# Value projections of the recurrent layers from two-part fp32r products, low weight parts by adding transfers, the inverse transposed into place, and a new order table

## The chip, the cores and the metric

The kernel runs on one core of one Trainium2 chip. The metric is device time in microseconds (us) of one execution; lower is better. The engines that matter are TensorE (PE, matrix products), VectorE (DVE), ScalarE (ACT), GpSimd (POOL) and SyncE (SP, which issues transfers).

## The reference

A residual trunk of four layers over 256 tokens of width 1024. The token mixers are RWKV-7, stick-breaking attention, sparse attention, RWKV-7; a SwiGLU feed-forward layer follows each. The change touches only the two RWKV layers (0 and 3):

```
xm  = h + (shifted - h) * mix                 # six mixes: r, k, v, w, a, g
r, k, v = xm[0:3] @ w_rkv                     # 1024 x 1024 each
decay, a, g from low-rank products of three other mixes
if layer 3: v = v + (v_first - v) * sigmoid(v0 + (xv @ v1) @ v2)
kk  = normalised (k * k_k);  k = k * (1 + (a - 1) * k_a)
state = state * w - (state.kk) (kk * a)^T + v k^T      # per token and head, 16 heads of 64
y     = state . r
out   = (group_norm(y) + (r.k.r_k) v) * g @ w_out
```

All inputs are float32. The recurrence is computed in chunks of 64 tokens.

## The kernel before, in words

The code doesn't issue instructions directly. It records them as operations in a `Plan`, in the order of the Python text. A long compressed table, `ORDER`, then says in which order they are issued over the whole program, which of the "any engine" operations (`anye`) go to DVE, ACT or POOL, and which buffer slot each tile gets. `emit` (line 546, so nearly every instruction carries that line) replays the table. Each engine takes its own instructions strictly in that order and waits at an instruction until its inputs are there. Where the table has an empty entry, `emit` issues `WARMERS` = 2 matmuls into an unused bank, `warm_o<-warm_x` (line 1572, 128x256 in bf16); no result depends on them.

Weights come in pieces of 512 KB (128 partitions x 1024 float32) as tiles `raw`, loaded by SP's queue. `piece` splits a piece into two fp32r tiles: `wh`, a rounding copy on any engine, and `wl = raw - wh`, a subtraction on DVE. `gemm2` multiplies with three fp32r products per tile (`mm3`: wh with the high part of the activations, wh with their low part, wl with the high part). The value projection alone, `vp`, is different before the change: `product` multiplies the float32 `raw` tile directly with the float32 activations `xv`, without any split. Slots are few: three for `wh`, three for `wl`.

An RWKV layer runs in this sequence (names are those of the profile):

- mixes of the normalised input on DVE (`xm`, `xr`, `xg`, `xv`), split into high and low halves (`kx` for keys, `prx` for r);
- key projection `kp` (piece `ahead` is one split earlier), low-rank `lora` products, the decay scan `L`, the r projection `rp`, which gives `PR`;
- `kss`, `ksd`, `kk`: key normalisation; then per pair of heads the scores `sc` on PE, which DVE masks into `SB`;
- `vp`, and from it `vf` (in layer 3 by way of `vd`), then transposes by matmul, `vtok`, and copies of them into `UV` for the products `bv`; `qct` fills `QC`;
- the inverse: eight small copies gather the 32x32 triangular blocks of `SB` into `E`, DVE transposes them into `inv`, and 31 steps of two DVE instructions each (`xtmp<-inv`, `inv<-inv,xtmp`) invert all blocks at once;
- DVE transposes the inverse to `xd` and, the other way, to `xw`; four copies `XT<-xw`, one for each group of 32 partitions, put `xw` into the larger matrix `XT`;
- `combine`: `cmb<-xd,SB` on PE, a copy `zs`, `cmb<-xw,zs` on PE, the result scaled into `XT`. It fills the off-diagonal block of each 64x64 inverse;
- the chain over the chunks (`xu<-u,XT`, `qu`, `pS`, `Y`), then the group norm, the gate (`pg` gives `gT`), and the output projection `po`.

`bn`, `prhl` and `pr` are the bonus term (r.k.r_k), and `am`, `EF`, `dc`, `Dt` belong to the decay.

Of the kernel before, what the change touches and what calls it, by code (L numbers as in the profile page):

```python
# [308 lines left out]
k{-II~7K%FccRBy3x!BJ(c;1U*;dauQ^j|f2=!A8r?36?px_Rwqi64gxnG%9K-
1|M(`IM_!^@WJEdYO4CKM(<b#RY#N`QIx3OuWNi2>Dp>2M_rD`<(N;{LTx`Z&C03Hs`1GJl^F`Ip5!Y^pNj;_mJ=K?N^`hkNClm^WpCd_|_Un93n0u_IoS  # L310
X#ec%~Eu6;|ViW%nv5r_poJDMvI2I6d)oKpsDzliy2&<KR2Gf|LznJ$CJs;B!wj7<oAI_I*HG!2P>Rh?3<3j$U@8KWivW|$NjIX7rOROm+u%u{Pi99<}7-
b^T%uFWZsS_E_IP!+?&&;S9l)~XN`a+{TJ5#4h;ju(K<hYNxi@S7#tu5R{y2ucR%>lxix5nIlpRG8oyQn)orn;;p+w)B(nylVnwHm83cb4_bE#_mP$MU<?
Hp{hG95;$ATgBY0$5_O48uM(01<VP#>jzvhxq=a6h&(9Lv3<s}y2{iLWr?)%$|HF>s-l@<z;_yCRR9llS#x^x1-
# [236 lines left out]
def trunk(ctx: ExitStack, tc: tile.TileContext, xT_in, vecs_in, wts, lora_in, consts_in, id32_in, outT, order, layers=None):  # L550
# [305 lines left out]
    def rwkv(j, layer, after):  # L856
# [39 lines left out]
        def product(key, x, name):  # L896

            out = bank(name, "g")
            for c in range(NC):
                if c % 4 == 0:  # L900
                    w = v3(raw_piece(key + (c // 4,)), 4)
# [833 lines left out]
```

## Time and profile before

| | |
|---|---|
| median of 3 runs | 1363.25 us (1361.84 to 1365.1) |
| the profiled execution | 1361.64 us, span 1359.9 us |
| PE busy | 1347.0 us, 99% of the span |
| DVE busy | 1120.4 us, 82% |
| ACT busy | 759.9 us, 56% |
| POOL busy | 11.4 us, 1% |
| transfers | 221.88 MB, 163 GB/s on average |
| granted PE clock | 1.000 |

Times in the profile count from the start of the span. A row of the timeline gives the start of a run of equal instructions, its length, the engine, line, operation, output and inputs with sizes, the count, and in square brackets how long the engine idled before it and on whose account. Matmuls overlap, so the length of a run of many is a better price than the length of one. A float32 matmul stands in the trace as two records. Layer 0's recurrent part lies at about 12 to 190 us, layer 3's at about 1000 to 1170 us.

### The profile page before, as it was taken

Reading aid. Unit: us, or ns where it says so; the run is one execution under the profiler, and the core shown is the slowest. Engines: PE = TensorE matmul, PEld = TensorE weight load, DVE = VectorE, ACT = ScalarE, POOL = GpSimd, SP = SyncE. Lnnn points to the kernel's source line nnn. Section 1 sums busy time; section 2 is a strip of 40 time slices with the busy share of each in tenths; the row PEclk is TensorE's granted clock in tenths of the full one; section 3 lists DMA queues with packets and bytes.
Section 4 is the critical chain, followed back from the end, with each engine's and each line's share of the span. In section 5 each row is a group of like instructions: output and inputs, shape, how many; then the busy total and the mean of one; then the engine's idle time right before and its main releaser. Section 6 shows DMA issues by size and latency. Waiting matters only on the chain.

```text
span 1359.9 us, 25662 instructions
## 1 busy us (share of the span) xinstructions
PE 1347.0 (99%) x10372; PEld 1179.5 (87%) x10372; DVE 1120.4 (82%) x1881; ACT 759.9 (56%) x1283; POOL 11.4 (1%) x18
## 2 busy tenths in 40 slices
PE   8999999999999999999999999999999999999998
PEld 8887798888888898888999798888897878988887
DVE  7998799775787888776799888876699997988754
ACT  5945566554335666554356965654249465666532
POOL 0000000000000000000000000000002000000000
PEclk9999999999999999999999999999999999999999
DMA  7332166655654367655656456666643321666554
GB/s 248 123 117 94 33 194 210 199 172 158 188 184 139 112 189 220 199 166 170 194 143 191 138 173 197 210 194 204 191 134 122 105 79 50 202 208 201 177 166 131
DMA packets 62854, 221.88 MB, mean 163 GB/s; under 512 B 7312, under 2 KB 8592, under 8 KB 62480
## 3 DMA queue, kind: packets, MB, share of 16 engines
q1 hardware_dynamic: 62736, 220.25, 52.3%
q8 instruction: 81, 1.33, 0.4%
q14 instruction: 37, 0.30, 0.1%
HBM read 217.08 MB, written 1.05 MB: 160 GB/s over the span
## 4 chain that ended last, share of the span: by engine, by line
PE 93%; DVE 3%; DMA 2%; ACT 2%; issue 0%; SPq 0%; DVEq 0%; ACTq 0%
PE dn L546 18%; PE up L546 17%; PE gate L546 17%; PE po L546 7%; PE qk L546 7%; PE vp L546 4%; PE kp L546 3%; PE rp L546 3%; PE vps L546 3%; PE z L546 2%; DMA raw<-in_wts_dram 1%; PE sc L546 1%; PE Y L546 1%; PE attn_o L546 1%; PE pg L546 1%; PE qi L546 1%
## 5 line engine op out<-in xcount | busy, mean ns | idle before, releaser
L546 DVE TENSOR_TENSOR wl<-raw,wh 128x1024 fp32r<-128x1024 f32 x285 | 347.7, 1222 | 98.8 <-ACT wh L546 96.3
L546 ACT CAST wh<-raw 128x1024 fp32r<-128x1024 f32 x237 | 248.7, 1050 | 202.1 <-PE dn L546 111.6
L546 PE MATMUL dn<-h,wh 128*128 128x512 f32 x704 | 244.2, 390 | 0.0
L546 PE MATMUL dn<-h,wl 128*128 128x256 f32 x704 | 198.5, 282 | 0.0
L546 PEld LDWEIGHTS dn<-h,wh 128*128 128x128 f32 x704 | 132.2, 188 | 27.7
L546 PE MATMUL gate<-xg,wring 128*128 128x512 f32 x704 | 133.2, 336 | 1.2 <-DVE wring L546 1.2
L546 PEld LDWEIGHTS dn<-h,wl 128*128 128x128 f32 x704 | 133.0, 189 | 0.0
L546 PE MATMUL up<-xg,wring 128*128 128x512 f32 x704 | 131.9, 336 | 0.0
L546 DVE TENSOR_TENSOR wring<-raw,wring 128x1024 fp32r<-128x1024 f32 x88 | 107.4, 1221 | 27.9 <-ACT wring L546 27.6
L546 PE MATMUL gate<-xg,wh 128*128 128x512 f32 x352 | 125.2, 392 | 0.0
L546 PE MATMUL up<-xg,wh 128*128 128x512 f32 x352 | 125.0, 392 | 0.0
L546 PEld LDWEIGHTS gate<-xg,wring 128*128 128x128 f32 x704 | 107.4, 188 | 16.0 <-DVE wring L546 1.5
L546 PEld LDWEIGHTS up<-xg,wring 128*128 128x128 f32 x704 | 107.4, 188 | 14.6
L546 ACT CAST wring<-raw 128x1024 fp32r<-128x1024 f32 x82 | 86.2, 1051 | 42.6 <-issue 16.5
L546 PE MATMUL gate<-xg,wl 128*128 128x256 f32 x352 | 98.4, 280 | 0.0
L546 PE MATMUL up<-xg,wl 128*128 128x256 f32 x352 | 98.4, 279 | 0.0
L546 PE MATMUL qk<-xg,wh 128*128 128x256 f32 (+1 forms) x384 | 91.5, 320 | 0.0
L546 PEld LDWEIGHTS up<-xg,wh 128*128 128x128 f32 x352 | 66.1, 188 | 14.6
L546 PEld LDWEIGHTS gate<-xg,wh 128*128 128x128 f32 x352 | 66.1, 188 | 14.4
L546 PE MATMUL qk<-xg,wl 128*128 128x256 f32 x256 | 71.7, 280 | 0.0
L546 PEld LDWEIGHTS qk<-xg,wh 128*128 128x128 f32 x384 | 63.5, 188 | 6.1 <-issue 0.8
L546 PEld LDWEIGHTS gate<-xg,wl 128*128 128x128 f32 x352 | 66.1, 188 | 0.0
(322 smaller groups left out, 2623.6 us busy)
## 6 DMA issues: line engine op xcount, KB each, us to landing
raw<-in_wts_dram SPq DMA_DIRECT2D x397, 512.0 KB, 3.7
lora<-in_lora_dram SPq DMA_DIRECT2D x2, 1536.0 KB, 8.3
rhl<-qa SPq DMA_DIRECT2D x32, 64.0 KB, 3.7
xt<-in_xT_dram SPq DMA_DIRECT2D x4, 256.0 KB, 4.3
lora<-in_lora_dram SPq DMA_DIRECT2D x2, 512.0 KB, 5.7
lg<-in_lora_dram SPq DMA_DIRECT2D x8, 128.0 KB, 3.6
inv<-in_id_dram SPq DMA_DIRECT2D x2, 512.0 KB, 3.3
out_dram<-xt SPq DMA_DIRECT2D x4, 256.0 KB, 4.0
```

The lines of the kernel that those rows point to most:

```text
L546: getattr(getattr(nc, o.eng), method)(*map(real, args), **{k: real(a) for k, a in kw.items()})
```

## The change

1. The value pieces are split as the others are. `wh` is the rounding copy as before. For keys in `ADDED`, `wl` isn't subtracted on DVE: ACT (or another engine) writes -wh into it, and a transfer issued by POOL reads the same piece from memory once more and adds it into `wl`. That is 16 transfers of 512 KB. The subtraction stays for all other weights.
2. `vp` uses `gemm2`, three fp32r matmuls in place of one float32 matmul: 384 matmuls in place of 128, which the trace counts as 256 records.
3. `xv` becomes two fp32r tiles, high and low. Each of the 16 mixes (128x256) is written to a scratch `xm`, then copied rounded into the high half and subtracted by DVE into the low half. The low half takes the slot group of `XT`, so `XT` is filled after the last use of `xv`.
4. `xw` goes. DVE transposes `inv` straight into the right-hand columns of `XT` (`XT<-inv`), the second `combine` product reads those columns, and two copies `XT<-XT` in place of four `XT<-xw` fill the left-hand columns.
5. In the code the value projection stands ahead of the inverse.
6. A new `ORDER` for the whole program. Besides order, it changes which engine has some of the free operations, and has 42 warming pairs for 30 (84 `warm_o` for 60).

```
+ADDED = ("rv",)
...
-c-rk+$&aK*R<9Q?wr|bMFTY$Xx5}(sYRjt1%-Z*^s;=&K@7-><-L?m}8{5N-
+c-rk+NpoY#aYokq>g@~ml^_-ZBtZZq2!a6j?q*L<uQR={XXy!PMl+*vNR};23RzM(!V#XZV-DU<KKky1BYd)NKIkX-U-
...
         anye.copy(h, r)
+        if key[0] in ADDED:
+            anye.scale(l, r, -1.0)
+            pool.dma_start(l, wts[i], accum_op=ALU.add)
+            return h, l
         dve.tensor_tensor(l, r, f(h), op=ALU.subtract)
...
-        xv = T([NC, S], "s1", "xv")
+        xv = [T([NC, S], g, "xv", F32R) for g in ("s1", "s0")]
...
             for i in range(c, c + 2):
-                mix(xv[:, i], "mv", i)
-                xvs.append(xv[:, i])
+                xvs.append(xm("mv", i))
+                split(xv[0][:, i], xv[1][:, i], xvs[-1])
...
-            vp = product(("rv", j, n), xv, "vp")
+            vp = gemm2(("rv", j, n), lambda c: (xv[0][:, c], xv[1][:, c]), "vp")
...
         dve.transpose(xd.rearrange("p u i -> p i u"), XI.rearrange("p t i -> p i t"))
-        xw = T([32, 32], "wh", "xw")
-        dve.transpose(xw.rearrange("p u t -> p t u"), XI)
-        for g in (1, 3, 0, 2):
-            r = slice(g * 32, (g + 1) * 32)
-            anye.copy(XT[r, :, g % 2 * 32:g % 2 * 32 + 32], xw[r])
+        dve.transpose(XT[:, :, 32:].rearrange("p u t -> p t u"), XI)
+        for r in (slice(0, 32), slice(64, 96)):
+            anye.copy(XT[r, :, :32], XT[r, :, 32:])
...
-                                  xr_[hi:hi + 32, c], start=True, stop=True)
+                                  X[hi:hi + 32, c, 32:], start=True, stop=True)
```

(`scale(l, r, -1.0)` is recorded with the source `raw` and an fp32r output, so it holds the rounded piece with its sign turned.)

On DVE, at the end of layer 0's inverse, this stands before:

```order
L546 COPY UV<-vtok 64x2x256
L546 TENSOR_TENSOR xtmp<-inv 128x112
L546 TENSOR_TENSOR inv<-inv,xtmp 128x4x28
L546 TENSOR_TENSOR xtmp<-inv 128x87
L546 TENSOR_TENSOR inv<-inv,xtmp 128x3x29
L546 TENSOR_TENSOR xtmp<-inv 128x60
L546 TENSOR_TENSOR inv<-inv,xtmp 128x2x30
L546 TENSOR_TENSOR xtmp<-inv 128x31
L546 TENSOR_TENSOR inv<-inv,xtmp 128x31
L546 TENSOR_TENSOR pr<-bn,vf_1119 128x512
L546 STREAM_TRANSPOSE xd<-inv 128x32x32
L546 STREAM_TRANSPOSE xw<-inv 128x32x32
```

and this now:

```order
L552 TENSOR_SCALAR prs<-pr,vecs 128x256
L552 TENSOR_TENSOR inv<-inv,xtmp 128x4x28
L552 TENSOR_TENSOR xtmp<-inv 128x87
L552 TENSOR_TENSOR inv<-inv,xtmp 128x3x29
L552 TENSOR_TENSOR xtmp<-inv 128x60
L552 TENSOR_TENSOR inv<-inv,xtmp 128x2x30
L552 TENSOR_TENSOR xtmp<-inv 128x31
L552 TENSOR_TENSOR pr<-bn,vf_1283 128x512
L552 TENSOR_TENSOR inv<-inv,xtmp 128x31
L552 STREAM_TRANSPOSE xd<-inv 128x32x32
L552 STREAM_TRANSPOSE XT<-inv 128x32x32
```

The three `UV<-vtok` copies that DVE made among the last steps (one is shown) are gone from it; ACT makes all of them now. A cast of `bonesr` and two small bonus instructions stand there instead.

On PE, ahead of the first `combine` of layer 0, before:

```order
L546 MATMUL vp<-xv,raw_1175 128x256 x8
L546 MATMUL vp<-xv,raw_1220 128x256 x8
L546 MATMUL vtok<-consts_192,vf_1119 64x64 x16
L546 MATMUL vtok<-consts_192,vf_1178 64x64 x16
L546 MATMUL qct<-consts_192,QC 128x64 x16
L546 MATMUL vtok<-consts_192,vf_1299 64x64 x16
L546 MATMUL vtok<-consts_192,vf_1294 64x64 x16
L546 MATMUL qct<-consts_192,QC 128x64 x16
L546 MATMUL bv<-UV,SB 64x64 x16
```

and now:

```order
L552 MATMUL vp<-xv,wl_1345 128x256
L552 MATMUL qct<-consts_543,QC 128x64 x16
L552 MATMUL vtok<-consts_543,vf_1483 64x64 x16
L552 MATMUL vtok<-consts_543,vf_1537 64x64 x16
L552 MATMUL bv<-UV,SB 64x64 x16
L552 MATMUL bn<-prhl,bonesr 128x512 x2
L552 MATMUL qct<-consts_543,QC 128x64 x16
L552 MATMUL bv<-UV,SB 64x64 x16
L552 MATMUL pg<-sg,lg 128x256 x2
L552 MATMUL pg<-sg,lg_1055 128x256 x2
L552 MATMUL cmb_1665<-xd,SB 32x32 x16
```

Half of the `vtok` matmuls now stand in the midst of `vp` instead of behind it; behind the last one come the same `bv`, `bn` and `pg` up to `cmb<-xd,SB`, without a warming pair. In layer 3 twelve warming matmuls precede `pg` there, and the two `bn` of 128x512, which followed the first `cmb` before, precede it as a group of four.

On POOL, what layer 0 has now (of the DMA rows only `raw`'s counterparts `wl` are new):

```order
L552 MEMSET Dt 128x32
L552 DMA wl_932<-in_wts_dram 128x1024
L552 COPY dc<-Dt 128x32
L552 DMA wl_1004<-in_wts_dram 128x1024
L552 DMA wl_1053<-in_wts_dram 128x1024
L552 DMA wl_1145<-in_wts_dram 128x1024
L552 DMA wl_1173<-in_wts_dram 128x1024
L552 DMA wl_1259<-in_wts_dram 128x1024
L552 DMA wl_1312<-in_wts_dram 128x1024
L552 DMA wl_1345<-in_wts_dram 128x1024
L552 MEMSET XT 32x32x32 x2
```

Before, only the `Dt` memset, the `dc` copy and the two `XT` memsets stood there; now eight transfers stand between them, and the `XT` memsets come behind the last.

More of the change, by code (lines that the diff above doesn't have):

```diff
@@ L309 @@
[L309 to L313, printed above, removed]
@@ new lines @@
+;rb;0R~E_dv2|Bx_`ct&oDn29d8`RaRCmUuG3MQx=(<cGGU!Z?yS0D!6I?Ukz?laMNzuO}l9~xP8-Z+D-evX_VgR;HLdH=a-
+w5bJK3xO}l9~?WX;1XMZO8mQMJPp_xM5rSyZ5$(&?B%1kC~$#D=$x$a49Ln|CaRv1`QpH)56Q%+I2wsOnLEY?(^;y3d7XUfavnz>TLEoO81MmZv{jNrYTG
+D0tkW|1Aa#n2ny4|2Xc7`Wzf-Zc))HD%g=VOWM?o0C7^Gpt=@dYh)<Yz(Z2-
+?uGe&Hg^?{>WOD?wb3tacoOt>wD6eRFo<iOyta#5ekumlF0H0;t3UA_tUV!!#5=3E`OAb7^{~`*;=_oK5+PEE@$_%g;F<{Yrk@O@8;ICO}-
+KqqgvFgN3~qE78dW!OW~|md{!uQ%ZqRvwZiNm{5(1c*CT6>H-e7e_glfLFPrO@U9U$@b;c_z&sL_}z3nwKD*MGPzg+Z-
+y+SolkIhxrEX++My}1z<U0U+pxfe;t-
@@ new lines @@
+j$XoKWmR%X^*9{%+)F?p)R)`%YuBM40%scdG1S3(%Z~t!RNVPagYu618Pq5W@~5X$Jy=dSdP@t{;nDfvfox4pKVl|{k~aVD|fr5YX4BRE?R1J)pS?PhN|1
+DdatS~nM$@?e&35eR)zCIkk7lh(|^mkkFrnPXh(zw{a0LagNlFJc7#nW!4#vCPDP9ICMSgEX)i}yQXzIgJQ9#xmyoDHh^>fCd}R{C8-
+kN&zEWvaAomkrMxQ|_Ac|z@;a)tK(Yi$ikWz^eFmq-OXc$rmi0^^RGOi;}=62>bdn3a#W`=`7sRUr0o$=FC#@JEF4uCEwko_5fJpkB+ogMrdjbLQK)>df?
+)aK^5V8ejU+db0mLYG6c-
+CTuL+E{^l9co0tumhz{SY0ndZ)Hv70jk*wlp`pHBmgj6>N_AT5)$Ys6C8pg1_Br^%bX%3LrMTbS(UI|7KAeLkxA={u!?L;Hb>nx3}rIIIFJk<>~-
+6)&enY22k*dm=0c;fChPxvBm`9W3J1aRjNLCCb-
@@ new lines @@
+=KDNoj)EPG8jb=@#U6E4gyN3>RzJ1)#n6Iww}Kb@&OwG-PjoCyQ}+B1?hC1vqCBu52+-
+HZ{z1ijHUq?XrxSeMDCjPHLR2GYu0bLUb@_HaXlfj2@9x2=XQZ?*>p#Sr-u<qv@Qk12J~dkMBzu=~(5DCG6;LL}o(Pr-
+&>B*nI~3bb!G(p%3v5&U{YDz7E=59RUjgZ)>2~WeC!Tz+NCu!=8T4|JO)Jr+Nl^=U5}iB0-
+QF+<qOmcYiJ1X4;q`uHxZ`wrPoG3rGZG>Qm3d&d8wwwWzs~GtI~}E2arMs-Tpo$f;x41=~gpHO;2kH_f_<ZDy9tqFJaG%yQn$kx3RJqiYy`0Wpn49(6G)3
+Vo;UIN`M7IKI#4wre|1$+7Lcjg9WIYQwAm)&Qjfkv!`QGUPZPw_(~SsY#WJdP)UKsp76ud8J(H>^Risf~rvI3J|LnUPcV21v=Ea2=k~9Hza-hGB-
+#aal3+H#0mT)Cvh|qflfX+)PUc2P;I985PrsO{(;4Rh6jUJ&Pzk#qk8)@{*+rEo1Z`8;-~aJdy{=bz9C-
@@ new lines @@
+gM}SZdOF?R%^z>X_LuD*2ME6TLEX{7bxRdswnu8Z=QMzFeKR~S2b3}+Tswail6^nml)`AWl<UlvSr_H+8oUHvFs3d7$EG-VpMU=M|{9Ay_h|rJZTJseJ;e
+z?3qIBRNfS=R*cw<$vW2gJyz>J-
+)EgY)@~oQS@{KwnzJDk8=G*_c)4DH+5)Q8vo^fbDns)CUyuTU+K*2F4>eI??i9lONj_u`qKM4#v_*aQkuGB}Jd_O<p1#D6E_hHXj!2Kcy9gz7M42<%2SGI
+C+ylB9!}UW#hcSe$gGQu>cmxsx5fGl>C`=NJ4H?@<BzlYPVrl|D=j5pdtclJ}a6u2KMm9XT$)gK-Q{De&^Goxq`GqF4{`0jA^B+3HbpKs1gP@HE_Ab%&G-
+#H(l=p2LVBOS|)Du|5)-+}^U5(@zLv(Q*By|g<^qAh!dLB!E7GhU{Z7?T`#LzUEJ`_^n3*m}_j)HE)Id{k0$vL>AK(i1`_xbqY?K005dA1jCcF0`Dawv-
@@ new lines @@
+NDPBuS5V0vhY#q#bg=L?**~a#)zQ^A5&u{fA<6S1)-
+6$<L7g_icS#AOqoj|eN?)Z~K_+8lAcKcVR$@N_C5=Ybi1IJ1k_1td7m($j`XLWo!<G$NxAgrFA^csM$67tYKnlahnM@{<KHAo0cqYi$lt6qh3ow!x(FeB>
+rB6;U2EM@a9tD_#z6P7_kuTkZ4bz*ji})t2C)-`XV?&d-R#yO%S*?yK1CPS04aL=UD6HU7AFA1A78=<I@*%-
+kc75<1B0S=55)<RwH6+PPqBQmsP8@w7NCwM`FhPp?WbvWGh>;bI{7o{m7*W+HiU_$t<lvTdN8*WCN#fjX5`5;YtID{UCKg;g%UQS$Zw5u$hRqfhtnhekdk
+vi0R&B55G~w0GN~Hnyj}GdvxerBUk{m#JUWW6mj>=Q^W`tN2Jj1dlt6Wo&3&X|uTgj80tg2&u5A_V>KF9QaY;p5BM!GZ8iH{iX!l6FyFutd_ab$4$f{A^^
+2`1m?@sa5OA#<PV)GseQ3@>}8mz-!Q;)@qC%ucD!cZ6Z8hWJ3mPdHrsj-
@@ new lines @@
+G9POY<Fm)pgb?<3~<@$#H7^+SOA(xq7;u>L4BxlR6hcUteD%cL%P|O~}hDu&>UINd{poSv+^`^|}935w5sg7vL8(8uuoeiN}!tzESdPHqAEH{8!&B2S7sW
+qB(wwe<1C;{1ppIuD!fuf5~n6A+VhBOJw?rjIiAPr3A|b;cDHbh9G@;Nx-%7DU)kU0elTDEfuk(AZ3!M?^l=wUek7}uB)DFQeD1Jy07mPUehMPm-
+PE}c5r1Sa%IzBJ@vKi!Pju8U+hoU%?X#LB-
+aeN6bG*U!P4)(thd*t`Pyo@Y+wD~RI!pX$Vi`ourVEb`pTPJIT60WUK$e`wurv9#0_&6$Eqgv55gNJD$N6#Aw=qFEaro+Xd-
+OFIgW0c@Zva_Ak^_R?D2_foMZ$v7mb*Zut;o}`dz|O`(fgjO!pu^jhcir!YD@pkrj?-h^6r>EhdvFFC#|GTX*9~riTj3<MFs-rt5`dp?LqA39=v(D3;HtD
+}j8dR+X-jm@w#NNb32NE(0+&Ix^srPy=<MC7_pZ0m&{<Ct6eS<-fiR)|*RKPMrbQN`}SCqRU}PS2|2zBlG33M1*vh{>7HVxYp%zX1x3rMK0--
@@ new lines @@
+(tlW_%SA3Jeo2yqx{lpxFBTlqAXI2axmrO>z?MT8C-
+HSPP4@x`&G~ZksSWgx_8XRjgzg4dzGJZ?#5>mKpIBW<SE@Oh=93g7Y3eV8Cb1}u_!=R0q<E&bwbo_owVFj5jFiQTq*F<1?APb$KAvcQxk8EzdRXEy>9C|L
+9j28ZyDUw)UQ!9xrXIDV0LWF0rZGjY$b`CXlem+iHHE}l`Dz?)9bHcs8rrcq3Mf+6X|(GHjLp;xJT`4CS!%}kAq6t+oJmKl(WSIY1E#2c$v%!V9^d-
+wSi*BJK4~D);Y)P98cf6n*MbQQHD+jNh)pi^-`=^FnxO?D#h1&7NNpbb6<K-
+<T$&!aV@Ygig`}?&g~u|+;_+DPNkWRbCIOUS0$h(Xx=gh(Op@g=PGISLu@5EMOze$lvK$tRmCj5|c14j(I;F0y3)d)`a7}lsIdYb6my@Lj#tuyqv&DEq6T
+nH3T5lxA|JWaRY+z&|6GUQ~A5H&2vy>-
+^#H(dvKf`cmX^hY~92q2zr9CHxKbG!M|Br=uRIKh8xl+H<xUf_qOKM|1U7K3(8o9(Sme_<R(#Algk(mn?laxuFsPx?i*C4IeM3+LO<|Kyq6w;ENB%Udl)<
@@ L365 @@
+T?#xTM+ziC)Zzg9K9Jq@_^$yi^6Awg}EiHxb)_@+;ts^`1mRtTCMs(%NQ;&SaU;Ac-
+#>Z8Sx$%N)EM7Taz)EXLC1u*9u6UCKdz0R;(_sy~6ul!7l){{;=QBF6
 """
@@ L894, in xm @@
             return t
[L896 to L901, printed above, removed]
-                with unit():
-                    for i in range(2):
-                        pe.matmul(out[:, i * S:(i + 1) * S], w[:, c % 4, i * P:(i + 1) * P], x[:, c, :],
-                                  start=(c == 0 and i == 0), stop=(c == NC - 1 and i == 1))
-            return out
         for c in range(0, NC, 2):
@@ L1056, in rwkv, with second @@
                 dve.tensor_tensor(SB[p // 4][:, hh ^ p % 2, :, p % 4], o[hh].rearrange("p (c a t) -> p c a t", c=NCH, a=2), masks, op=ALU.mult)
+        act.activation(sga, sga, AF.Sigmoid)
+        act.activation(sgb[:64], sgb[:64], AF.Sigmoid)
+        lg = [T([S], "xm", "lg") for i in range(4)]
+        for i in range(4):
+            sp.dma_start(lg[i], lora_in[j][:, 4096 + i * S:4096 + (i + 1) * S])
+            plan.after(plan.ops[-1], [mixed])
+        lg1 = T([2 * S], "sqa", "lg1")
+        sp.dma_start(lg1, lora_in[j][:, 5120:5120 + 2 * S])
+        def second(out, p, r0, stop):
+            r = slice(r0 + (p % 2) * 32, r0 + (p % 2) * 32 + 32)
+            pe.matmul(out, lg1[r, (p // 2) * P:(p // 2 + 1) * P], sgb[r], start=(r0 > 0), stop=stop)
+        for n in range(4):
+            vp = gemm2(("rv", j, n), lambda c: (xv[0][:, c], xv[1][:, c]), "vp")
+            vps = ab(vp)
+            Vn = vfirst[n]
+            if j == 0:
+                anye.copy(Vn, vps)
+                continue
+            pv_ = bank("pv"), bank("pv")
+            with unit(2):
+                for i in range(2):
+                    second(pv_[i][:, :S], 2 * n + i, 64, True)
+            sv, d_ = t2("sv"), t2("vd")
+            for i in range(2):
+                act.activation(sv[:, i], pv_[i][:, :S], AF.Sigmoid, bias=vec("v0", 2 * n + i))
+            dve.tensor_tensor(d_, Vn, vps, op=ALU.subtract)
+            dve.tensor_tensor(d_, d_, sv, op=ALU.mult)
+            dve.tensor_tensor(Vn, d_, vps, op=ALU.add)
         E = T([32, 32], "wh", "E")
@@ L1091, in rwkv @@
             dve.tensor_tensor(c8(pr[:, p:p + 2]), pairs(PR, p)[:, :, 1], pairs(QC, p)[:, :, 1], op=ALU.mult)
-        act.activation(sga, sga, AF.Sigmoid)
-        act.activation(sgb[:64], sgb[:64], AF.Sigmoid)
-        lg = [T([S], "xm", "lg") for i in range(4)]
-        for i in range(4):
-            sp.dma_start(lg[i], lora_in[j][:, 4096 + i * S:4096 + (i + 1) * S])
-            plan.after(plan.ops[-1], [mixed])
-        lg1 = T([2 * S], "sqa", "lg1")
-        sp.dma_start(lg1, lora_in[j][:, 5120:5120 + 2 * S])
-        def second(out, p, r0, stop):
-            r = slice(r0 + (p % 2) * 32, r0 + (p % 2) * 32 + 32)
-            pe.matmul(out, lg1[r, (p // 2) * P:(p // 2 + 1) * P], sgb[r], start=(r0 > 0), stop=stop)
-        for n in range(4):
-            vp = product(("rv", j, n), xv, "vp")
-            vps = ab(vp)
-            Vn = vfirst[n]
-            if j == 0:
-                anye.copy(Vn, vps)
-                continue
-            pv_ = bank("pv"), bank("pv")
-            with unit(2):
-                for i in range(2):
-                    second(pv_[i][:, :S], 2 * n + i, 64, True)
-            sv, d_ = t2("sv"), t2("vd")
-            for i in range(2):
-                act.activation(sv[:, i], pv_[i][:, :S], AF.Sigmoid, bias=vec("v0", 2 * n + i))
-            dve.tensor_tensor(d_, Vn, vps, op=ALU.subtract)
-            dve.tensor_tensor(d_, d_, sv, op=ALU.mult)
-            dve.tensor_tensor(Vn, d_, vps, op=ALU.add)
         for p in range(0, NC, 2):
```

80 lines of the change are left out of this document (23 added, 57 removed).

## The prediction

> **What bounds the kernel now.** I read the page first (its head, the chain that ended last, the costliest groups), then tables of windows around the two recurrent layers, then the timelines of PE and DVE there.
>
> ```profile
> span 1359.9 us, 25662 instructions
> PE 1347.0 (99%) x10372; PEld 1179.5 (87%) x10372; DVE 1120.4 (82%) x1881; ACT 759.9 (56%) x1283; POOL 11.4 (1%) x18
> ...
> PE 93%; DVE 3%; DMA 2%; ACT 2%; issue 0%; SPq 0%; DVEq 0%; ACTq 0%
> ...
> L546 PE MATMUL gate<-xg,wring 128*128 128x512 f32 x704 | 133.2, 336 | 1.2 <-DVE wring L546 1.2
> ```
>
> Over the program PE looks like the only bound: 1347.0 of 1359.9 us, 93% of the chain. But that is an average over stages. The windows below (time, length, then PE, PE loads, DVE, ACT and POOL busy, clock, DMA share, GB/s) cut out the part ahead of the inverse and the inverse itself, in layers 0 and 3.
>
> ```profile
> 12.00:92.00 80.00, 80.00 (x639) 70.34 (x638) 78.87 (x143) 56.26 (x95) 2.90 (x5) 1.00 0.45 146
> 92.00:126.00 34.00, 33.24 (x372) 27.54 (x370) 30.33 (x76) 16.04 (x30) 0.00 (x0) 1.00 0.41 129
> ...
> 1000.00:1072.00 72.00, 71.95 (x618) 63.37 (x617) 71.35 (x127) 51.30 (x88) 7.01 (x4) 1.00 0.32 104
> 1072.00:1109.00 37.00, 36.64 (x397) 30.76 (x395) 35.29 (x86) 16.98 (x33) 0.00 (x0) 1.00 0.39 122
> ```
>
> There DVE is as full as PE: 78.87 of 80 us, 71.35 of 72, and nearly full through the inverse. Two engines are saturated side by side, so taking work from PE alone uncovers DVE. That decides the forecast.
>
> **The value GEMM on PE.** The lengths come from starts of consecutive rows of the timeline:
>
> ```profile
> 100.57 15.19 PE L546 MATMUL vp<-xv,raw 128*128 128x256 f32 x68
> 115.69 1.16 PE L546 MATMUL vtok<-consts,vf 64*64 64x64 f32 x64
> ...
> 1087.72 14.08 PE L546 MATMUL vp<-xv,raw 128*128 128x256 f32 x64
> 1101.73 1.16 PE L546 MATMUL vtok<-consts,vf 64*64 64x64 f32 x64
> ...
> 29.37 7.28 PE L546 MATMUL kp<-kx,ahead 128*128 128x256 f32 x60
> 36.49 0.40 PE L546 MATMUL kp<-kx,wh 128*128 128x256 f32 x2
> ...
> L546 PE MATMUL vp<-xv,raw x256: 379/379/483, 82.4 to 1101.4; 128*128 128x256 f32 x128
> ```
>
> A float32 record costs (115.69 - 100.57)/68 = 0.222 us, in layer 3 14.01/64 = 0.219. An fp32r matmul of the same shape, in `kp`, costs (36.49 - 29.37)/60 = 0.119. Now 256 x 0.221 = 56.6 us; then 384 x 0.119 = 45.7. PE gains 10.9 us, 5.4 in each layer.
>
> The 24 added warming matmuls cost PE about 0.11 each, from
>
> ```profile
> 5.73 0.93 PE L1572 MATMUL warm_o<-warm_x 128*128 128x256 bf16 x7
> 8.73 1.13 PE L546 MATMUL ss<-sq,ones 128*128 128x256 f32 x4 [2.07 <-DVE eps_rms L546]
> ...
> 8.00:9.00 1.00, 0.27 (x1) 0.27 (x2) 1.00 (x3) 0.00 (x0) 0.00 (x0) 1.00 1.04 395
> ```
>
> (0.93 us for 7, the last one's tail of 0.27 taken off). That is 2.6 us, and nearly all of it lies in front of things that PE has to wait for, so I charge none except the two at the start (0.2). PE's own work falls by some 8 to 11 us. If nothing else bound it, that would be the gain.
>
> **DVE up to the inverse.** Counting the rows of DVE ahead of `inv<-E`, layer 0 gains eight `xv<-xm,xv` subtractions and loses seven small instructions (three `am`, one `kx`, one `prx`, one `QC`, one `sg`). The value weights cost DVE nothing before and nothing now: their low parts go by ACT and POOL. The nearest row for the new subtraction, same shape, and two of those lost:
>
> ```profile
> 36.29 0.43 DVE L546 TENSOR_TENSOR kx<-xm,kx 128x256 fp32r<-128x256 f32 x1
> 36.63 1.22 DVE L546 TENSOR_TENSOR wl<-raw,wh 128x1024 fp32r<-128x1024 f32 x1
> ...
> 39.95 0.42 DVE L546 CAST prx<-xr 128x512 fp32r<-128x512 f32 x1
> ...
> 47.64 0.40 DVE L546 TENSOR_SCALAR am<-EF,vecs,omka 128x256 f32<-128x256 f32 x1
> ```
>
> From start to start the subtraction is 0.34 us: 8 x 0.34 = +2.7. Off go three `am` and about four more at 0.3 to 0.6, some 2.2. So `inv<-E` comes +0.5 us in layer 0 if DVE stays full; the same count gives +0.5 in layer 3.
>
> **DVE from `inv<-E` to `xd`.** In layer 0:
>
> ```profile
> 102.50 0.42 DVE L546 CAST prhl<-prs 128x512 fp32r<-128x512 f32 x1
> ...
> 104.47 0.35 DVE L546 TENSOR_SCALAR prs<-pr,vecs 128x256 f32<-128x256 f32 x1
> ...
> 117.51 0.68 DVE L546 COPY UV<-vtok 64x512 f32<-64x512 f32 x1 [0.53 <-ACT UV L546]
> 118.12 0.30 DVE L546 TENSOR_TENSOR xtmp<-inv 128x156 f32<-128x156 f32 x1
> ...
> 120.76 0.69 DVE L546 COPY UV<-vtok 64x512 f32<-64x512 f32 x1 [0.84 <-ACT UV L546]
> ...
> 124.25 1.98 DVE L546 STREAM_TRANSPOSE xd<-inv 128x1024 f32<-128x1024 f32 x1
> 126.12 1.91 DVE L546 STREAM_TRANSPOSE xw<-inv 128x1024 f32<-128x1024 f32 x1
> ...
> 126.38 0.69 PE L546 MATMUL cmb<-xd,SB 32*32 32x32 f32 x32 [0.40 <-DVE xd L546]
> ```
>
> Three `UV` copies go to ACT: 3 x 0.61 = 1.8 (117.51 to 118.12), and with them two waits, 0.53 + 0.84 = 1.4. One `prhl` cast goes (0.35). One `prs` (0.3) and a `bonesr` cast (at most 0.35, since it is a quarter of that `prhl` cast; 0.2 taken) come. Sum -3.1; with the +0.5, `xd` is ready 2.6 us earlier. PE waited 0.40 us there even before, so it follows DVE fully: PE would reach `cmb` about 5 us earlier than before, at 119 to 121 us, and wait to about 123.8 us. Layer 0 up to `cmb`: -2.6, bounds -4.5 (DVE's +0.5 goes away because ACT took over more) to 0 (ACT, which now makes all eight `UV` copies, is as late as it was).
>
> In layer 3 nothing of that kind leaves:
>
> ```profile
> 1105.48 0.69 DVE L546 COPY QC<-qct 128x512 f32<-128x512 f32 x1
> ...
> 1106.78 2.00 DVE L546 STREAM_TRANSPOSE xd<-inv 128x1024 f32<-128x1024 f32 x1
> ...
> 1108.04 1.76 PE L546 MATMUL pg<-sg,lg 128*128 128x256 f32 x8
> 1109.73 0.44 PE L546 MATMUL cmb<-xd,SB 32*32 32x32 f32 x16
> ```
>
> The `QC` copy goes, one `pr` and one `prhl` come: net +0.6, so `xd` ends at +1.1. PE had no wait at 1109.73, since `xd` had ended at 1108.78; it has 0.95 us of slack, and four `bn` matmuls (about 1.2 us) now come ahead of `cmb` instead of behind. I take `cmb` +0.8 and 1.2 less behind it: -0.4, bounds -2 and +1.5.
>
> **Transposing into place.** One transpose for another: 1.91 us either way (bounds 1.9 and 3.8 for the strided output, which no row shows). Two copies `XT<-XT` replace four, which lie beside `combine`. `cmb<-XT` needs only the transpose. Counting DVE's rows behind `xd` in the same way gives -0.3 in layer 0 and -0.8 in layer 3, bounds -1.5 and +1 each.
>
> **ACT.** It takes the 16 `wl<-raw` (taken as its `wh` cast of the same shape, 1.05 us) and the `xv` casts (a quarter of that size, so 0.3 to 1.05; 0.4 taken). Of layer 0's share one `wl` and seven `xv` casts stand ahead of the last `ksd`, with some of the small operations that left DVE: 1.05 + 2.8 + about 1, say +5 us. ACT's waits there cover this barely:
>
> ```profile
> L546 ACT CAST wh<-raw 128x1024 fp32r<-128x1024 f32 x237 | 248.7, 1050 | 202.1 <-PE dn L546 111.6
> ...
> 78.42 0.69 ACT L546 ACTIVATE ksd<-kss,lim 128x512 f32<-128x512 f32 x1 [5.09 <-PE kss L546]
> ...
> 84.56 3.31 ACT L546 COPY E<-SB 32x512 f32<-32x512 f32 x3 [3.53 <-DVE SB L546]
> ```
>
> 5.09 + 3.53 us of idling against +5: hidden. If `kss` came late too, `ksd`, `kk`, `sc` and the whole DVE queue behind it would slip; price 0 to +2, 0 taken.
>
> **The adding transfers.** No row shows one. The nearest are SP's loads of the same size, and for POOL's issue the rows of a small copy, once alone and once among full DVE work:
>
> ```profile
> raw<-in_wts_dram SPq DMA_DIRECT2D x397, 512.0 KB, 3.7
> ...
> 55.90 0.27 POOL L546 COPY dc<-Dt 128x32 f32<-128x32 f32 x1 [20.02 <-ACT Dt L546]
> ...
> 1038.58 4.95 POOL L546 COPY dc<-Dt 128x32 f32<-128x32 f32 x1 [11.50 <-ACT Dt L546]
> ```
>
> Landing costs 3.7 us if it is like a load; with the DMA share at 0.45 or less, the extra 8.4 MB fit. Eight issues must feed PE's 192 matmuls (22.8 us) and some 4 us of `qct` and `vtok` between them, 27 us in all, with about 5 us of head start from free `wl` slots: an issue may take (27 + 5)/8 = 4.0 us before PE waits for it. The bounds are 0.27 and 4.95; I take about 1, nearer the row without disturbance, as 4.95 is one instruction. The `XT` memsets now stand on POOL behind all eight, ahead of the chain only, and hide.
>
> The Trainium skill, page "SBUF — State Buffer", section "Who interferes with whom", states that GpSimd is shut out of the port it shares with VectorE while VectorE runs a two-port copy or cast, and that a two-input VectorE instruction only blocks a GpSimd one that reads SBUF. By that rule the stretched `dc` copy is a reader's case, and an issue that writes descriptors waits only for copies and casts, so it speaks for the low bound; the 4.95 us row agrees with it, though no run here shows an issue.
>
> **Elsewhere** the table moves instructions in places that PE fills. The one stall that the page names there, 1.2 us for `wring`, may go or stay; -0.3 with the start's +0.2 taken in.
>
> **Sum.** Layer 0: -2.6 - 0.3; layer 3: -0.4 - 0.8, of which I hold back 0.5, as PE's queue there ends in `vf`, `vtok`, `UV`, `bv`, all behind DVE; elsewhere -0.3. That is -3.9 on the profiled 1361.64 us, so 1357.7. That execution lies 1.6 us under the median of 1363.25 (its span of 1359.9 leaves 1.7 us around it), so as a median I expect 1359.3.
>
> **The rivals.**
> - *PE pays in full.* If DVE can go ahead by as much as PE (its waits in layer 3 or at `SB` were really PE's), the whole 10.9 less 2.6 of warming matmuls shows: -8 to -9, 1354.7. For it: PE is at 80.00 of 80. Against: DVE idles just 1.13 us in that window. 0.10.
> - *Nothing to measure.* ACT's +5 us and layer 3's +1.1 us eat the 2.6: within 2 us, 1362.7. For it: ACT's thin cover. 0.25.
> - *POOL's issues stretch.* At 4.95 us each, eight take 39.6 us against 32: `vp` ends 7.6 us late. In layer 0, PE would reach `cmb` at about 127.4 against 126.38, +1.0; in layer 3, where `vp` would have ended some 4.7 us earlier, +2.9 ahead of `vf`, and `wl` slots held that long delay `po`'s pieces by some more: +4.5, 1367.7. It decides from 4.0 us an issue. 0.13.
> - *The clock.* PE idled 2.07 us ahead of 8.73 us, and the granted clock stayed 1.00 (the window of 8 to 9 us above). In layer 0 it now waits 3 to 5 us ahead of `cmb` with no warming pair. If that dropped the clock for about as long as the wait, the work behind it would lose some 1.7 us (half of 3.4): 1361.0. 0.05.
>
> On that last one, the Trainium skill, page "TensorE: Matmul & The Clock Gate", Part 1, says the clock halves after an idle window of about 3.4 us; by it a 4 us wait could cost that, a 2 us one not. Here the 2.07 us row agrees, and no run shows a longer wait.
>
> **Chances.** My case has 0.47. A measurement tells a change of 0.2%, 2.7 us. Of my case 0.40 lies beyond that, with the first rival and 0.02 of the others: faster 0.52. Same: 0.07 of mine, 0.21 of "nothing", 0.03 of the clock: 0.31. Slower: the stretched issues and 0.04 of "nothing": 0.17. The range 1354.7 to 1366.3 takes in the full payment at one end and a mild stretch at the other; my own case spans 1356.5 to 1361.5.
>
> **What the next profile would show.** If I am right: `vp` as 384 records of 0.119 us pitch; DVE still without idle time up to `inv<-E`; PE idle 2 to 5 us before layer 0's first `cmb`, for `xd`; `xd` at about 121.7 us; `cmb` without the `XT` copies in its way; POOL's issues near 1 us. I am wrong if PE waits for `wl` in `vp`, if DVE idles ahead of `inv<-E` (then ACT or PE sets it), or if the clock falls below 1.00 behind `cmb`.

## The result and the profile after

The changed kernel takes 1373.54 us (median, 1370.50 to 1373.88) against 1364.17 for the kernel before beside it (1361.84 to 1366.10): a ratio of 1.0069, 95% interval 1.0054 to 1.0084. It is slower by 0.7%, some 9 us, where 4 us less had been forecast. These lines of the page answer those of before; PE's share of the chain that ended last falls from 93% to 79%, DVE's rises from 3% to 5% and that of transfers from 2% to 4%:

```profile
span 1371.7 us, 26075 instructions
PE 1345.2 (98%) x10524; PEld 1182.0 (86%) x10524; DVE 1130.5 (82%) x1904; ACT 779.8 (57%) x1319; POOL 22.8 (2%) x34
...
PE 79%; DVE 5%; DMA 4%; ACT 2%; issue 1%; DVEq 0%; ACTq 0%; SPq 0%; POOLq 0%
```

The same windows as before, columns as there:

```profile
12.00:92.00 80.00, 80.00 (x645) 70.83 (x644) 78.31 (x143) 65.45 (x114) 4.23 (x6) 0.99 0.54 165
92.00:126.00 34.00, 29.11 (x429) 26.76 (x427) 28.60 (x77) 27.75 (x42) 6.20 (x7) 1.00 0.83 206
...
1000.00:1072.00 72.00, 72.00 (x602) 63.91 (x602) 71.70 (x131) 59.30 (x107) 4.37 (x5) 1.00 0.39 118
1072.00:1109.00 37.00, 32.73 (x337) 29.85 (x336) 32.33 (x76) 25.39 (x37) 4.61 (x6) 0.95 0.83 199
```

In the stretch of `vp` and the inverse both PE and DVE now idle (29.11 and 28.60 of 34 us). The resource that filled up is the transfer engines: share 0.83, where it was 0.41 and 0.39. The clock column of layer 3 shows 0.95. PE's waits, the queues (packets, MB, share of sixteen engines' span) and the issues of the changed kernel:

```profile
PE vp L552 <- DMA wl<-in_wts_dram: 5.6, 5, 1.8
PE ss L552 <- ACT sq L552: 2.1, 1, 2.1
PE vp L552 <- ACT wh L552: 1.8, 1, 1.8
PE vp L552 <- ACT vf L552: 1.6, 1, 1.6
...
PE qk L552 <- DVE qa L552: 1.1, 1, 1.1
PE pT L552 <- DVE prs L552: 0.8, 1, 0.8
...
PE ss L552 <- DVE ssr L552: 0.7, 1, 0.7
...
q1 hardware_dynamic: 62736, 220.25, 51.4%
q0 software_dynamic: 2304, 8.39, 3.4%
...
wl<-in_wts_dram POOLq DMA_DIRECT2D x16, 512.0 KB, 7.2
```

An adding transfer lands 7.2 us after its issue, a load of the same size takes 3.7 over the program. The queue lines show that the engines are slower at it: q1 moves 220.25 MB in 51.4% of 1371.7 us, 312 GB/s while busy; q0 moves 8.39 MB in 3.4%, 180 GB/s. In the trace's packet records the median packet of 4096 B takes 159 ns in a load and 328 ns where it adds. That alone doesn't make up the difference in landing: a transfer has 128 such packets, eight for each of the 16 engines if they are spread evenly, so an estimate from these packet times is 2.6 us for 1.3. The rest is probably waiting among other packets on engines that are 0.83 busy; no run takes it apart. Loads suffer with them: `raw` lands after 7.2 us in the window of 92 to 126 us, 3.5 before.

### The profile page after: what moved, and what is told of

It reads as the page before. It is cut to its first block, busy times and chain, and to the rows that moved or that the text cites. A ratio compares the mean times of both kernels' runs of the same rounds, so it can differ in the third digit from the quotient of the medians.

```text
span 1371.7 us, 26075 instructions
## 1 busy us (share of the span) xinstructions
PE 1345.2 (98%) x10524; PEld 1182.0 (86%) x10524; DVE 1130.5 (82%) x1904; ACT 779.8 (57%) x1319; POOL 22.8 (2%) x34
## 3 DMA queue, kind: packets, MB, share of 16 engines
q1 hardware_dynamic: 62736, 220.25, 51.4%
q0 software_dynamic: 2304, 8.39, 3.4%
## 4 chain that ended last, share of the span: by engine, by line
PE 79%; DVE 5%; DMA 4%; ACT 2%; issue 1%; DVEq 0%; ACTq 0%; SPq 0%; POOLq 0%
PE dn L552 18%; PE up L552 17%; PE gate L552 16%; PE po L552 6%; PE qk L552 4%; DMA raw<-in_wts_dram 2%; PE z L552 2%; PE rp L552 2%; PE kp L552 2%; PE vps L552 2%; DMA wl<-in_wts_dram 2%; DVE wl L552 1%; PE vp L552 1%; PE Y L552 1%; PE pg L552 1%
## 5 line engine op out<-in xcount | busy, mean ns | idle before, releaser
L552 PE MATMUL up<-xg,wring 128*128 128x512 f32 x704 | 134.7, 336 | 0.0
L552 ACT COPY gus<-gate 128x256 f32<-128x256 f32 x88 | 32.5, 373 | 69.2 <-PE gate L552 68.8
```

The costliest lines, as they stand in the source:

```text
L552: getattr(getattr(nc, o.eng), method)(*map(real, args), **{k: real(a) for k, a in kw.items()})
```

## The experiments

**Which part of the change costs.** Four kernels that ran together, on the changed kernel's order.

Without the transfers:

```
+        out = [o for o in out if o is None or o.role != "add"]      # drops the 16 POOL transfers
```

> The changed kernel without its 16 adding transfers: wl keeps the value that ACT wrote, so the low weight parts of the value projection are not computed. Theory of the transfers (adding packets of 4096 B take 328 ns against 159 ns of a load, the transfers land 7.2 us after issue, and PE waits for wl inside vp): all waits of vp for a DMA go, layer 0 gains about 1.5 us and layer 3 about 4 to 5, together -5 to -7 on the changed kernel, 1366.5 to 1368.5. What is left against the kernel before (+3 to +4) lies in places of the order that the change did not have to touch: the start, layers 1 and 2, the last feed-forward layer. Rival, the order table alone: vp waits for its ACT rows in the same places, within 2 us of the changed kernel, 1372 to 1375.

Measured: 1361.26 us, ratio to before 0.9977 (0.9967 to 0.9988). Against the changed kernel's median that is 12.3 us (by the two ratios 0.92%, 12.5 us), twice what I expected. Without the transfers the rest of the change gains 1.5 us by the medians of this group, 3.1 by the ratio.

The same transfers without adding:

```
-            pool.dma_start(l, wts[i], accum_op=ALU.add)
+            pool.dma_start(l, wts[i])
```

> The 16 transfers are kept on POOL's queue with the same bytes, but overwrite instead of adding (wl then holds the raw piece, so the low parts are wrong). It tells the adding apart from the software queue. If adding is what is slow: packets at about 159 ns, landing 4 to 5 us, and most of the gain of the run without transfers, 1367 to 1370. If issuing by POOL is what is slow: landing stays above 6 us and the time within 2 us of the changed kernel, 1372 to 1375.

Measured: 1362.55 us, 0.9993 (0.9980 to 1.0006). The software queue is as fast as SP's, or nearly: packets at 174 ns, and

```profile
q0 software_dynamic: 2304, 8.39, 2.0%
...
wl<-in_wts_dram POOLq DMA_DIRECT2D x16, 512.0 KB, 4.2
```

Same bytes, same queue, same order, and by the medians 1.3 us over no transfer at all (2.2 by the ratios). So some 10 to 11 of the 12.3 us are due to adding, not to issuing by POOL.

The low parts by DVE, at the place of ACT's copy:

```
+            o.eng, o.instrs = "vector", [("tensor_tensor", (l, r, h), {"op": ALU.subtract})]
```

> The low parts by a subtraction on DVE at the place of ACT's copy (1.22 us each, eight in each recurrent layer), without the copies and the transfers. If DVE is the bound there, as the prediction had it, 9.8 us a layer are added to a full queue, less what idle time DVE now has between inv and xd: 8 to 14 us over the run without transfers, 1375 to 1381. If DVE is not the bound, the time is that of the run without transfers, 1366.5 to 1369.

Measured: 1389.10 us, 1.0184 (1.0163 to 1.0205), 27.8 us over the run without transfers, for 16 x 1.22 = 19.5 us of DVE work, twice the most that I expected. PE's longest waits there:

```profile
PE vp L561 <- DVE vf L561: 4.9, 1, 4.9
PE sc L561 <- DVE SB L561: 3.3, 3, 1.7
PE vp L561 <- DVE wl L561: 3.3, 3, 2.4
```

DVE is a bound, as the prediction had it; and behind PE's long waits the granted clock halved (0.82 in 126 to 165 us, 0.88 in 1072 to 1109). The trace's clock record has half speed for 27.3 us in all in the two layers, which could cost up to 13.7 us. That is the likely reason why the loss exceeds the work; it was not tested.

The value projection back in one float32 matmul, with no low parts and no transfers:

```
+                plan.ops[-1].instrs = [("matmul", (out[...], f(wh[...]), f(xs(c)[0])), {...}) for i in range(2)]
```

> The value projection by one float32 matmul in place of three fp32r ones (0.221 us a record, 256 records, against 384 at 0.119), with wh and the high part of xv as operands, so the low parts are left out; ACT's copies and the transfers go too. The rest is the changed kernel. PE does 5.4 us more in each layer than in the run without transfers. If DVE's chain through inv to xd is the bound, most of that is hidden: within 3 us of that run. If PE is the bound: 8 to 11 us slower than that run, 1375 to 1379.

Measured: 1367.62 us, 1.0035 (1.0021 to 1.0049), 6.4 us over the run without transfers by the medians, 7.9 by the ratios. So the 10.9 us less of PE work are worth 6.4 to 7.9 when nothing but ACT's copies is paid for them: more than the theory of DVE alone allowed, less than PE in full.

**The dose.** Half of each adding transfer, its packets unchanged:

```
+            pool.dma_start(l[:64], wts[i][:64], accum_op=ALU.add)
```

> The changed kernel with the adding transfers cut to 64 of 128 partitions (the low parts of the other half are left out): half the packets, each still 4096 B and adding. If the time of the adding packets on the transfer engines is what costs (full: 47 us of all sixteen engines and 12.3 us of the kernel's time; none: 0), landing falls from 7.2 us to 4.5 to 5.5 and the time to a third to a half of that loss, 1363 to 1367. If each transfer has a fixed delay through POOL and its queue, landing stays above 6 us and the time above 1370.

Measured: 1362.88 us, 0.9997 (0.9987 to 1.0008).

```profile
q0 software_dynamic: 1280, 4.20, 1.8%
...
wl<-in_wts_dram POOLq DMA_DIRECT2D x16, 256.0 KB, 4.3
```

Still 328 ns a packet, but half of them, and all but 1.6 of the 12.3 us are gone (by the ratios all but 2.7 of 12.5), just below the range I gave. The cost isn't proportional to the bytes. The `wl` slots offer an account of this, which is worked out and was not tested by itself. A slot is taken for ACT's copy (1.06 us), the landing, and the 24 matmuls of the piece (24 x 0.119 = 2.86). With three slots and 7.2 us a piece can come every (1.06 + 7.2 + 2.86)/3 = 3.7 us, with 4.2 or 4.3 us every 2.7. In `vp` alone PE would take one every 2.86. POOL's rows in layer 3 of the changed kernel show the slow pace, and two of the run with plain transfers, below them, the pace there:

```profile
1084.34 0.86 POOL L552 DMA_DIRECT2D wl<-in_wts_dram  x1 [12.04 <-ACT wl L552]
1086.96 0.86 POOL L552 DMA_DIRECT2D wl<-in_wts_dram  x1 [1.76 <-ACT wl L552]
1089.91 0.86 POOL L552 DMA_DIRECT2D wl<-in_wts_dram  x1 [2.09 <-DMA wl<-in_wts_dram]
1095.48 0.86 POOL L552 DMA_DIRECT2D wl<-in_wts_dram  x1 [4.71 <-ACT wl L552]
...
1076.52 0.53 POOL L552 DMA_DIRECT2D wl<-in_wts_dram  x1 [9.74 <-ACT wl L552]
...
1086.07 0.53 POOL L552 DMA_DIRECT2D wl<-in_wts_dram  x1 [3.89 <-ACT wl L552]
```

Three intervals take 1095.48 - 1084.34 = 11.1 us with adding, 3.7 each, and 1086.07 - 1076.52 = 9.6 us without, 3.2 each, since PE has `pv`, `qct` and warming matmuls between the pieces; the interval behind them is 3.1 against 2.8. Each issue with adding takes 0.86 us here; none is stretched. The account fits the changed kernel and the runs with plain and with half transfers; more slots were not tried.

In layer 0 the slots are the smaller part. There PE waits 1.3 us for `wl`, but 1.8 us for `wh` and 1.6 us for `vf`. Both are ACT's, which has idled 3.85 us for a late `raw` shortly ahead of that `vf` (1.99 at the same place in the run without transfers). The delay then reaches DVE, for `pr<-bn,vf` stands ahead of the inverse's last instruction and of `xd` in DVE's order, and `bn` is computed by PE behind `vp`. In the changed kernel:

```profile
103.32 1.06 ACT L552 ACTIVATE wl<-raw 128x1024 fp32r<-128x1024 f32 x1 [3.85 <-DMA raw<-in_wts_dram]
...
124.53 0.69 DVE L552 TENSOR_TENSOR pr<-bn,vf 128x512 f32<-128x512 f32 x1 [2.30 <-PE bn L552]
```

How the 12.3 us divide between slots, late loads and the clock is not shown.

**The clock.** In the changed kernel's trace PE waits 1.83 us for `wl` in layer 3, and then (the last row is a window, columns as above):

```profile
1081.19 0.38 PE L552 MATMUL vp<-xv,wl 128*128 128x256 f32 x1 [1.83 <-DMA wl<-in_wts_dram]
...
1084.07 0.41 PE L552 MATMUL vp<-xv,wl 128*128 128x256 f32 x1
1084.28 0.63 PE L552 MATMUL vp<-xv,wh 128*128 128x256 f32 x2
...
1082.00:1086.00 4.00, 4.00 (x24) 4.00 (x22) 1.53 (x5) 3.01 (x5) 0.86 (x1) 0.57 0.23 65
```

Three matmuls take 0.64 us from start to start (1084.07 to 1084.71) in place of 0.36. The trace's clock record has half speed for 3.413 us there, and once more at the start, behind a wait of 2.1 us for `sq`. Warming matmuls put into both waits:

```
+WAITS = 37
...
+        for o, n in ((ss, 8), (vp[WAITS], 6)):
+            out[out.index(o):out.index(o)] = [None] * n
```

> The changed kernel with warming matmuls put into two waits of PE: 16 ahead of the fourth ss at the start (about 1.8 of 2.1 us) and 12 ahead of the unit of vp in layer 3 that waits 1.8 us for wl. In the changed kernel's trace 3.4 us at half clock follow each of these waits. Theory of the clock: both stretches go, the start gains about 1 us, layer 3 at most 1.7, 1370.5 to 1372.5. If the transfers are what sets vp's pace in layer 3, PE only waits longer for the next wl there, and little but the start's microsecond shows: 1372 to 1373.5.

Measured: 1369.74 us, 1.0052 (1.0038 to 1.0065), 3.8 us under the changed kernel by the medians, but 2.3 by the ratios, whose intervals overlap; the two were not timed together, so a gain is not shown. Both stretches are gone, and layer 3 from the first `kp` to the first `po` costs 3.9 us more than before in its profile instead of 5.3. At the start the warming matmuls are not shown to be the reason: the execution with one instruction moved (the last experiment) has none of them there and no half speed either, and reaches the last `kp` of layer 0 earlier, at 41.8 us against 43.6. And half speed came up elsewhere in the run with warming matmuls, in layer 0, behind a wait that was longer there:

```profile
109.41 0.79 PE L558 MATMUL vp<-xv,wh 128*128 128x256 f32 x2 [4.36 <-ACT vf L558]
...
108.00:112.00 4.00, 2.59 (x12) 2.59 (x13) 3.73 (x11) 4.00 (x7) 1.36 (x2) 0.50 0.66 119
```

The clock makes the waits dearer, and its stretches lie at other places from run to run; it isn't the first cause.

**Parts of the change alone.** On the kernel before, the inverse transposed in place:

```
+        plan.ops[-1].instrs = [("transpose", (XT[:, :, 32:].rearrange("p u t -> p t u"), XI), {})]
...
+            plan.ops[-1].role = "skip" if g % 2 else (XT[r, :, :32], XT[r, :, 32:])
```

> The kernel before with one part of the change alone: the inverse transposed straight into XT, two copies XT<-XT in place of four XT<-xw, combine reading XT; its own order, float32 value product. If the copies behind xd are on the way to the chain's end, as the prediction had it by -0.3 and -0.8 us a layer, 1361 to 1362.5. If they lie beside other work, no difference within 1 us of the kernel before.

Measured: 1363.33 us, 1.0003 (0.9993 to 1.0012). Nothing to be measured: in its profile `inv<-E` to the first `po` of layer 0 takes 0.2 us less than before, in layer 3 0.1. And on the kernel before, the three `UV` copies of layer 0 given to ACT:

```
+        for o in uv:
+            o.eng, o.instrs = "scalar", [o.alts["scalar"][0]]
```

> The kernel before with one part of the new table alone: the three UV<-vtok copies of layer 0 that DVE makes among the last steps of the inverse are made by ACT. The prediction counted 3.2 us for them on DVE (1.8 of copies, 1.4 of waits). If DVE alone set the first cmb of layer 0, it would come 2 to 3 us earlier, 1360 to 1361. If PE, which with the float32 products reaches cmb only 0.4 us before xd is ready, is as much a bound, no more than 0.5 us shows: within 1 us of the kernel before.

Measured: 1362.41 us, 1.0003 (0.9990 to 1.0016). No gain, and DVE's rows at the end of the inverse show why, before and in this run:

```profile
123.42 0.19 DVE L546 TENSOR_TENSOR inv<-inv,xtmp 128x31 f32<-128x31 f32 x1
123.64 0.69 DVE L546 TENSOR_TENSOR pr<-bn,vf 128x512 f32<-128x512 f32 x1
...
120.44 0.19 DVE L550 TENSOR_TENSOR inv<-inv,xtmp 128x31 f32<-128x31 f32 x1
123.79 0.69 DVE L550 TENSOR_TENSOR pr<-bn,vf 128x512 f32<-128x512 f32 x1 [3.17 <-PE bn L550]
124.40 1.99 DVE L550 STREAM_TRANSPOSE xd<-inv 128x1024 f32<-128x1024 f32 x1
```

DVE is through the inverse 3.0 us earlier (120.44 against 123.42), near the 3.2 that were counted. But `pr<-bn,vf`, which stands ahead of `xd` in its order, then waits 3.17 us for `bn` on PE, though `xd` isn't made from `pr`. So `xd` starts when it did before (124.40 against 124.25), and so does `cmb`, to which PE now comes with no wait (126.38 before):

```profile
124.76 1.76 PE L550 MATMUL pg<-sg,lg 128*128 128x256 f32 x8
126.54 0.69 PE L550 MATMUL cmb<-xd,SB 32*32 32x32 f32 x32
```

In this order `xd` can't come before PE's `bn`, so taking work from DVE alone gives nothing. An order with `pr` behind `xd` was not run.

**The low parts by POOL's own subtraction:**

```
+            o.eng, o.instrs = "gpsimd", [("tensor_tensor", (l, r, h), {"op": ALU.subtract})]
```

> The low parts by a subtraction on POOL (two inputs in SBUF) in place of ACT's copy and the transfer; the computation is complete. If POOL takes about 2.5 us for 128x1024 and doesn't disturb DVE, eight take 20 us a layer beside vp: near the run without transfers, 1361 to 1364. If it is stretched beside DVE as the dc copy was (4.95 us against 0.27 before), or holds DVE up, 40 us a layer: slower than the changed kernel, 1376 to 1400.

Measured: 1395.98 us (1391.80 to 1399.79), 1.0244 (1.0218 to 1.0269). POOL takes 2.3 to 2.8 us each, not 5, and it is still slower than all others, for it holds DVE up:

```profile
98.50 7.18 POOL L561 TENSOR_TENSOR wl<-raw,wh 128x1024 fp32r<-128x1024 f32 x3 [14.61 <-ACT wh L561]
...
101.09 2.32 DVE L561 TENSOR_TENSOR inv<-inv,xtmp 128x31 f32<-128x31 f32 x1
103.45 2.31 DVE L561 TENSOR_TENSOR xtmp<-inv 128x60 f32<-128x60 f32 x1
105.79 0.22 DVE L561 TENSOR_TENSOR inv<-inv,xtmp 128x60 f32<-128x60 f32 x1
```

An instruction of the inverse with 31 elements takes 2.32 us beside it, 0.19 otherwise, and one with 60 takes 2.31 for 0.22.

**The order outside the recurrent layers.** One DVE instruction of the sparse attention layer moved up:

```
+        out.remove(o)                       # the second prs<-prs,sm on DVE
+        out.insert(out.index(qa), o)        # ahead of qa<-rhl
```

> The changed kernel with one instruction moved in the sparse attention layer: DVE's second prs<-prs,sm ahead of the qa<-rhl in front of it, which waited 1.18 us for a transfer and held it up. If the order there is what costs, PE's wait of 0.8 us for prs goes and the layer's end comes 0.5 to 1 us earlier against its start; if the late transfer hits something else behind it, the end stays where it was within 0.3 us. Nothing is expected in layers 0 and 3.

Measured in a single execution: 1371.88 us. From the first `gate` of the feed-forward layer ahead of it to that of the one behind it the changed kernel needs 2.0 us more than the kernel before, this one 1.3. PE waited 0.81 us for `prs` there (first row, the changed kernel); in the moved order (second row) the three matmuls follow one another:

```profile
758.34 0.44 PE L552 MATMUL pT<-consts,prs 128*128 128x128 f32 x2 [0.81 <-DVE prs L552]
...
755.99 0.49 PE L561 MATMUL pT<-consts,prs 128*128 128x128 f32 x3
```

So up to 0.7 us of it is that place, within the half to one that I had expected. It is one execution against one: the run without transfers, with the old place, needs 1.6 us there, so some of the 0.7 may be the difference between executions.

## Why the prediction was wrong, step by step

By first instructions of stages, in profiles of single executions (us against the kernel before):

| stage | run without transfers | changed kernel | changed kernel, one instruction moved |
|---|---|---|---|
| start to the last `kp` of layer 0 | -0.9 | +1.2 | -0.9 |
| layer 0, to the first `po` | -3.7 | -0.4 | +0.5 |
| to the last `kp` of layer 3 | +1.6 | +3.2 | +1.6 |
| layer 3, to the first `po` | +0.8 | +5.5 | +6.1 |
| to the end | +1.7 | +2.4 | +2.9 |
| sum | -0.6 | +11.8 | +10.2 |

In the two layers, where the transfers run, the two executions with them need 8.0 and 9.5 us more than the one without. The 2.1 us at the start lie ahead of the first transfer (78.14 us): there the changed kernel's execution has a longer wait for `sq` (2.1 us for 1.2) and the half-speed stretch, which the execution with the moved instruction has not.

- **The adding transfers, charged at nothing.** This is the step that failed. I priced an adding transfer like a load, 3.7 us to landing, and said that with the DMA share at 0.45 or less the extra 8.4 MB fit. For plain transfers that held (1.3 us). Adding ones land in 7.2 us, with twice the engine time per packet (328 ns against 159), and the share went to 0.83. I also asked only what POOL's issue could cost and worked out 4.0 us an issue as the limit; I did not ask how long a `wl` slot is held. At 3.7 us landing a piece could come every 2.5 us, at 7.2 every 3.7, where PE takes one every 2.86 in `vp` alone. The step costs 12.3 us by the medians, 8.0 to 9.5 of them seen in the two layers; between the forecast change of -3.9 us and the measured +9.4 lie 13.3. PE's waits for `wl` in `vp`, 5.6 us, are the first sign that the prediction named for being wrong.
- **The rival of stretched issues** ended on the right side, with a wrong mechanism: issues took 0.86 us (one 1.00) beside a DVE that was 78.31 of 80 us busy up to 92 us and 28.60 of 34 behind that. The passage of the Trainium skill that I quoted ("SBUF — State Buffer", "Who interferes with whom") held: writing descriptors did not suffer from DVE's two-input instructions. What it says of a GpSimd instruction that reads is what the POOL subtraction showed, with DVE as the one that waits (2.32 us for 0.19).
- **DVE binds the inverse, and layer 0 gains 2.9.** Right in the size, where the transfers are left out: -3.7. Up to `inv<-E` it is -0.2, where +0.5 had been forecast, and behind `xd` -0.3. `inv<-E` to `xd` went from 30.6 us (93.62 to 124.25) to 27.5 (92.44 to 119.97 in the run without transfers), -3.1 as the sum of rows gave. But PE was not far ahead: I forecast a wait of 3 to 5 us for `xd` ahead of `cmb`, and it is 0.43 us,

```profile
119.90 1.76 PE L554 MATMUL pg<-sg,lg 128*128 128x256 f32 x8 [0.44 <-DVE pr L554]
...
122.09 0.69 PE L554 MATMUL cmb<-xd,SB 32*32 32x32 f32 x32 [0.43 <-DVE xd L554]
```

  since PE begins `vp` 2.2 us later in the new order (84.62 against 82.42) and on its way waits 0.8 us for `wh`, 0.4 for `QC` and 0.4 for `pr`. I also took it that PE follows DVE there, and left out that DVE follows PE: `pr<-bn,vf`, ahead of `xd` in DVE's order, waits for PE's `bn`, 3.17 us in the `UV` run, 2.51 in the float32 run, 2.30 in the changed kernel. The float32 run and the `UV` run show both sides: PE's saving alone is worth 6.4 to 7.9 of 10.9 us in the new order, DVE's alone nothing in the old one.
- **Layer 3, -0.7.** Measured +0.8 without transfers, inside the bounds given, on the wrong side of zero.
- **In-place transposing, -0.3 and -0.8.** No gain shown: -0.2 and -0.1 in the profile, and the -1.1 us of both together lie just outside the interval of the ratio (0.9993 to 1.0012).
- **Elsewhere, -0.3.** Measured -0.9 at the start, but +1.6 and +1.7 behind the two layers, with the transfers out of the way: +2.4 in all. I named one stall and let the rest of a wholly new table pass at nothing. Waits that the old order did not have (`qk` for `qa`, `pT` for `prs`, `ss` for `ssr`) are 1.1, 0.8 and 0.7 us in the changed kernel; moving one instruction gained up to 0.7 us at `prs`. What the rest of it is due to stays open.
- **The clock.** I gave it 0.05, ahead of layer 0's `cmb`, from a wait of 3 to 5 us. It came at other places and after shorter waits: half speed for 3.4 us behind waits of 1.8 and 2.1 us, and none behind the 2.07 us that I quoted. By the Trainium skill ("TensorE: Matmul & The Clock Gate", Part 1) the clock goes to half after an idle window of about 3.4 us. The trace doesn't agree with a wait of that length as the condition, since half speed came behind a wait of 1.83 us here.
- **PE's price of `vp`** was right: 0.119 us a matmul.

Without the transfers the prediction of 1359.3 would have stood 2 us under 1361.3. That is nearer than its terms were: layer 0 came out 0.8 us better than forecast, layer 3 1.5 and the rest 2.7 worse, so the nearness would have been luck in part. No kernel of this study whose computation is complete beats the kernel before: what the change saves on PE it has to pay on DVE (+27.8), on POOL (+34.7) or on the transfer engines (+12.3) for the low parts.

## What to carry to other kernels

A transfer that adds is not a load: here it took twice the engine time per packet. Look at the DMA share of the very stretch where it runs, not of the program. For a stage fed through a few slots, work out how long one slot is held (writer, flight, reader), divide by the number of slots, and compare with the consumer's pace; here the loss was 1.3 to 1.6 us where the slots kept up and 12.3 where they did not. Before work is taken from one engine, look in its order for an instruction that waits for another engine: here `pr<-bn,vf` ahead of `xd` gave back all that DVE had saved.
